# Softmax weights through diagonal matrices, six dense columns with an unsplit float32 second layer, one norm chain for three tiles

## The chip, the core and the metric

One core of a Trainium2 chip runs the kernel. The metric is the device time of one execution in microseconds (us). The engines are TensorE (PE, with its weight load PEld), VectorE (DVE), ScalarE (ACT), GpSimd (POOL) and the DMA queues; SP issues most transfers, POOL the gathers by index.

## The reference, cut to what matters

512 tokens of width 1024 pass through one decoder layer: attention with three branches beside a state-space group, then a layer in which each token chooses 128 of 16384 experts.

```
z = rms_norm(h, attn_norm);  proj = z @ w_in
p_s = masked_softmax(q @ k_sel);  p_w = masked_softmax(q @ k_win)
a = g0 * (p_c @ v_c) + g1 * (p_s @ v_sel) + g2 * (p_w @ v_win)
h = h + concat([a, s5(u)]) @ w_out
x = rms_norm(h, ffn_norm)
eidx, gate = top 16 of 256 key pairs, for each of 8 heads
act = gelu(x . u_tab[eidx]) * gate
h = h + sum over the chosen experts of act * v_tab[eidx]
out = rms_norm(h, final_norm)
```

## The kernel before

Tokens are cut into four tiles of 128 (`T` = 0 to 3).

**Attention.** `attention(T)` goes through four groups, two sets of heads `g` by two branches `br`. `scores` makes the scores of four heads, takes their maximum on DVE (`nm`), their exponential on ACT (`Pt`, with the sum `sm`), turns `sm` into gate over sum, and multiplies each head's `Pt` by it: on DVE for T < 3, on ACT for T = 3 (`PSC`). `pv` then takes 128 x 128 blocks of `Pt`, four heads to a PSUM bank, transposes them with the identity on PE, copies the bank to SBUF and multiplies by the values. There are T + 1 blocks for each head, so tile 1 has 32 transposes, tile 2 has 48, tile 3 has 64.

**Experts, two ways.** Tiles 0 and 1 (`SPARSE`) gather the rows of their chosen experts by index. A step takes one expert for each of 128 tokens: a gather of 1 MB, a dot product on DVE (`junk<-X`), a gelu on ACT, and a sum on DVE (`X<-X,act`) or, for the last 20 steps of tile 0, on PE by a diagonal matrix (`dg`, built on ACT from the identity, two matmuls a step). The 128 steps of tile 0 (`peer`) run between the attention and routing of tiles 1 to 3; the 128 of tile 1 (`Steps`) run in the dense loop, one a column.

Tiles 2 and 3 (`DENSE`) compute all 16384 experts in `dense`, 128 columns of 128 experts, with a gate of zero where an expert is not chosen. Column j loads two 512 KB halves (u and v) into a ring of three `raw` buffers, and splits each half into a float32r high part (`hi`, ACT) and low part (`lo`, DVE). The first layer (`hid`) is 24 matmuls of 256 columns. After gelu and gate the activations are split too (`acthi` on ACT, `actlo` on DVE), and the second layer (`outp`) is 12 float32r matmuls of 512 columns into four banks `acc` that stay open for the whole loop. A `raw` half is released, and the next load issued, when its `lo` is done. For j < 64 the gates of columns 64 to 127 are made beside the loop, one group every second column: one-hot tables on DVE, 16 small matmuls on PE.

**Order.** Before the loop the order on each engine comes from a scheduler. Inside it the order is the program's (`ordered`): iteration j holds `hid(j + 1)`, the step of tile 1, `gated(j + 1)`, `actlo(j + 1)`, `outp(j)`, `lo(j + 1, 1)`. An engine works in order; semaphores tie the engines together.

**End.** `final` is an RMS norm: a square with sum on ACT, then a chain of 14 small DVE operations (`rms`, with `rsqrt`), a scaling of 128 x 1024, and the store. Its small tiles (`f_s`, `f_r`) have two buffers, and three tiles (1, 2, 3) go through it after the loop.

Of the kernel before, what the change touches and what calls it, by code (L numbers as in the profile page):

```python
# [12 lines left out]
F32 = mybir.dt.float32  # L13
# [3 lines left out]
I32 = mybir.dt.int32  # L17
U32 = mybir.dt.uint32
AF = mybir.ActivationFunctionType
ALU = mybir.AluOpType  # L20
# [143 lines left out]
def hymba_kernel(ctx: ExitStack, tc: tile.TileContext, a, out, dbg=None):  # L164
# [520 lines left out]
    kcF, vcF = ct("kcF", [128, 2, 31]), ct("vcF", [31, 2, 64])  # L685


    PSC = lambda T, h: T > 2
    PCP = lambda T, kb: T < 3 and kb % 2
    AT, ST, XN, EI, GA = {}, {}, {}, {}, {}  # L690

    def attention(T):
        N = 128 * (T + 1)
        n31 = 7 if T == 0 else 31
        kcT, vcn = (kc0, vc0) if T == 0 else (kcF, vcF)
        ob = bank()
        O = b3(ob, 128)

        pcs = [bank(), bank()]
        for h in range(8):  # L700
            rows = slice(64 * (h % 2), 64 * (h % 2) + 64)
            PE.matmul(b3(pcs[h % 2], 128)[:, h // 2, 0:n31], qT[T][rows, h // 2], kcT[rows, h // 4], start=True, stop=True)
        scl = M.S()
        sc = scl.v([128, 8, n31])
        mx = tiny.tile([128, 8], F32, name="mx")
        sh = [128, 8, n31]
        for par in range(2):
            V.tensor_tensor(sc[:, par::2], b3(pcs[par], 128)[:, :, 0:n31], cmpb[:, T, 0:1, 0:n31].to_broadcast([128, 4, n31]), op=ALU.add)
        bfree(*pcs)
        V.reduce_max(mx, sc, axis=AX.X)  # L710
        V.tensor_tensor(sc, sc, mx[:, :, None].to_broadcast(sh), op=ALU.subtract)
        S.activation(sc, sc, AF.Exp)
        V.tensor_tensor(sc, sc, cmpb[:, T, 1:2, 0:n31].to_broadcast(sh), op=ALU.mult)
        V.reduce_sum(mx, sc, axis=AX.X)
        V.tensor_scalar(mx, mx, 1e-30, None, op0=ALU.max)
        V.reciprocal(mx, mx)
        V.tensor_tensor(mx, mx, gts[:, T, :, 0], op=ALU.mult)
        V.tensor_tensor(sc, sc, mx[:, :, None].to_broadcast(sh), op=ALU.mult)
        yield

        def scores(g, br):
            pl = M.S() if T == 0 else M.L((0, 1))
            Pt = pl.v([128, 4, N])
            nm = tiny.tile([128, 4], F32, name="nm")
            sm = tiny.tile([128, 4], F32, name="sm")
            for h in range(4):
                par, i = h % 2, h // 2
                ps = bank()
                rows = slice(64 * par, 64 * par + 64)
                PE.matmul(ps[:, 0:N], qT[T][rows, 2 * g + i], KT[rows, 2 * br + g, 0:N], start=True, stop=False)  # L730
                PE.matmul(ps[:, N - 128:N], identb, maskb, start=False, stop=True)
                V.reduce_max(nm[:, h:h + 1], ps[:, 0:N], axis=AX.X, negate=True)
                S.activation(Pt[:, h], ps[:, 0:N], AF.Exp, bias=nm[:, h:h + 1], accum_out=sm[:, h:h + 1])
                bfree(ps)
            V.tensor_scalar(sm, sm, 1e-30, None, op0=ALU.max)
            V.reciprocal(sm, sm)
            V.tensor_tensor(sm, sm, gts[:, T, 4 * g:4 * g + 4, 1 + br], op=ALU.mult)
            for h in range(4):
                if PSC(T, h):
                    S.activation(Pt[:, h], Pt[:, h], AF.Copy, scale=sm[:, h:h + 1])  # L740
                else:
                    V.tensor_scalar(Pt[:, h], Pt[:, h], sm[:, h:h + 1], None, op0=ALU.mult)
            return pl, Pt

        def pv(g, br, pl, Pt):
            for kb in range(T + 1):
                b = bank()
                pt = b3(b, 128)
                for h in range(4):
                    PE.transpose(pt[:, 2 * (h % 2) + h // 2], Pt[:, h, kb * 128:kb * 128 + 128], ident)  # L750
                ps = M.S()
                PT = ps.v([128, 4, 128])
                if PCP(T, kb):
                    V.tensor_copy(PT, pt)
                else:
                    S.activation(PT, pt, AF.Copy)
                bfree(b)
                for par in range(2):
                    PE.matmul(O[64 * par:64 * par + 64, 2 * g:2 * g + 2], VC[:, kb, 128 * br + 64 * g:128 * br + 64 * g + 64],
                              PT[:, 2 * par:2 * par + 2], start=(br == 0 and kb == 0), stop=False, skip_group_check=True)  # L760
                M.free(ps)
                yield
            M.free(pl)

        prev = None
        for g in range(2):
            for br in range(2):
                cur = (g, br) + scores(g, br)
                yield
                if prev:  # L770
                    yield from pv(*prev)
                    if prev[1] == 1:
                        yield from cmp_pv(prev[0], sc, vcn, O, n31)
                prev = cur
        yield from pv(*prev)
        yield from cmp_pv(1, sc, vcn, O, n31)
        M.free(scl)
        al = M.S()
        aT = al.v([128, 4, 128])
        S.activation(aT, O, AF.Copy)  # L780
        bfree(ob)
        AT[T] = (al, aT)
        tap(f"aT{T}", aT)
        yield
# [430 lines left out]
    def dense(xh, xl, sp):  # L1215
# [15 lines left out]
        def load(n):  # L1231
            if ring[n] and nload[n] < NE:
                raw, j = ring[n].popleft(), nload[n]
                nload[n] += 1
                SP.dma_start(raw, a["uvt"][j][:, half[n]])
                loaded[n][j] = raw

        def hi(j, n):
            if j < NE:
                S.activation(his[j % 2][:, half[n]], loaded[n][j], AF.Copy)  # L1240

        def lo(j, n):
            if j < NE:
                o = half[n]
                V.tensor_tensor(los[j % 2][:, o], loaded[n][j], his[j % 2].bitcast(F32)[:, o], op=ALU.subtract)
                ring[n].append(loaded[n].pop(j))
                load(n)

        def hid(j):
            if j < NE:  # L1250
# [16 lines left out]
                V.tensor_tensor(g, g, gates_of(j), op=ALU.mult)  # L1267

        def acthi(j):
            if j < NE:  # L1270
                S.activation(acts[j % 2][:, 0], gS[j % 2], AF.Copy)

        def actlo(j):
            if j < NE:
                act = acts[j % 2]
                V.tensor_tensor(act[:, 1], gS[j % 2], act.bitcast(F32)[:, 0], op=ALU.subtract)

        def outp(j):
            (ah, al), vh, vl = (acts[j % 2][:, i] for i in range(2)), his[j % 2][:, D:], los[j % 2][:, D:]
            for t in range(2):  # L1280
                ts = slice(128 * t, 128 * t + 128)
                for i, (l, r) in enumerate(((ah, vh), (ah, vl), (al, vh))):
                    for n in range(2):
                        PE.matmul(acc[2 * t + n], l[:, ts], r[:, 512 * n:512 * n + 512], start=(j == 0 and i == 0),
                                  stop=(j == NE - 1 and i == 2), skip_group_check=True)
# [23 lines left out]
        with ordered("V", "S", "PE", "G"):  # L1309
            gated(0)  # L1310
            acthi(0)
            actlo(0)
            next(ngp)
            for j in range(NE):
                gp, ngp = ngp, gate_group(j)
                step = sp.k < 128 and (j + 1) * n > done * SPREAD
                hi(j + 2, 0)
                hi(j + 1, 1)
                next(gp, None)
                next(ngp, None)  # L1320
                if step:
                    sp.dot()
                hid(j + 1)
                if step:
                    sp.gelu()
                lo(j + 2, 0)
                gelu(j + 1)
                next(gp, None)
                gated(j + 1)
                next(gp, None)  # L1330
                acthi(j + 1)
                if step:
                    sp.add()
                    done += 1
                actlo(j + 1)
                outp(j)
                lo(j + 1, 1)
                if sp.k == 128 and step:
                    final(sp.T, xs[sp.T], junk)
                if j == 100:  # L1340
                    for i in range(2):
                        SP.dma_start(row(7)[:, half[i]], hsave[i])
        assert sp.k == 128
        for i, T in enumerate(DENSE):
            xs[T] = row(7)[:, half[i]]
            for n in range(2):
                V.tensor_tensor(xs[T][:, 512 * n:512 * n + 512], acc[2 * i + n], xs[T][:, 512 * n:512 * n + 512], op=ALU.add)
            final(T, xs[T], raws[i][:, 0:D])


    proj_k(0, w_k[1], G)
# [299 lines left out]
```

## Time and profile before

| | us |
|---|---|
| median of three runs (1617.03 to 1622.68) | 1618.69 |
| profiled execution, its own time | 1620.03 |
| profiled execution, span from first to last instruction | 1618.2 |
| DVE busy | 1475.7 |
| PE busy | 1367.1 |
| ACT busy | 837.0 |

The span is what the trace covers; the time of the same execution is 1.8 us longer. Busy time counts an engine's instructions as they lie in the trace, where those that follow each other overlap a little.

### The profile page before, as it was taken

What the parts mean: (1) busy time and instruction counts of PE and PEld (TensorE: products, weight loads), DVE (VectorE), ACT (ScalarE), POOL (GpSimd) and SP (SyncE); (2) the same over time, 40 slices, a digit from 0 to 9 for tenths busy, and PEclk for the clock granted to TensorE, in tenths of its full rate; (3) what the DMA queues carried; (4) which work ended last, traced back from release to release, by engine and by line L of the source; (5) the groups of instructions that cost most, each with busy time, mean ns of one, the idle gap of its engine ahead of it and who ended that gap; (6) DMA issues with size and microseconds to landing.
All of it is one profiled execution on the core that took longest, in us unless ns stands there. A gap on an engine that the chain in (4) does not pass through costs nothing.

```text
span 1618.2 us, 24071 instructions
## 1 busy us (share of the span) xinstructions
PE 1367.1 (84%) x8256; PEld 1081.8 (67%) x8256; DVE 1475.7 (91%) x3392; ACT 837.0 (52%) x2046; POOL 521.8 (32%) x383
## 2 busy tenths in 40 slices
PE   5687794588946689696579999999999999999996
PEld 2366572454433455682358888888888999999995
DVE  8986279969899999699999999999999999999998
ACT  2335523545455675225565555555555556555553
POOL 6422013745354233003002333333333433333331
PEclk9897898787877789899859999999999999999998
DMA  6331478888998989309707999999999999999994
GB/s 263 104 105 65 169 278 295 330 321 300 375 352 297 345 356 370 152 6 343 248 4 262 338 345 332 342 337 340 333 346 357 392 375 377 374 375 379 375 376 171
DMA packets 88967, 469.45 MB, mean 290 GB/s; under 512 B 10253, under 2 KB 10893, under 8 KB 50701
## 3 DMA queue, kind: packets, MB, share of 16 engines
q0 software_dynamic: 37152, 268.98, 42.7%
q1 hardware_dynamic: 51692, 198.94, 34.3%
q8 instruction: 64, 1.05, 0.2%
q14 instruction: 59, 0.48, 0.1%
HBM read 464.74 MB, written 3.15 MB: 289 GB/s over the span
## 4 chain that ended last, share of the span: by engine, by line
DVE 46%; PE 29%; issue 12%; DMA 6%; ACT 3%; POOL 3%; SPq 0%; DVEq 0%; POOLq 0%; ACTq 0%
PE bank L134 29%; DVE X L134 27%; DVE lo L134 8%; DVE junk L134 7%; DMA X<-in_uv,eidx 5%; POOL X L134 2%; ACT X L134 2%; DVE act L134 1%; DVE nm L134 1%; DVE more L134 1%; DMA X<-in_x 0%; ACT gt L134 0%; DMA raw<-in_uvt 0%; DVE zT L134 0%; DVE hid L134 0%
## 5 line engine op out<-in xcount | busy, mean ns | idle before, releaser
L134 POOL DMA_INDIRECT X<-in_uv,eidx x256 | 431.6, 1686 | 967.0 <-DVE X L134 854.1
L134 ACT ACTIVATE X<-bank 128x256 f32<-128x256 f32 (+5 forms) x423 | 213.4, 518 | 184.0 <-PE bank L134 134.3
L134 PE MATMUL bank<-hi,act 128*128 128x512 f32 x1024 | 299.7, 394 | 0.0
L134 PE MATMUL bank<-XH,hi 128*128 128x256 f32 x1024 | 288.9, 282 | 4.1 <-ACT hi L134 4.1
L134 PE MATMUL bank<-XH,lo 128*128 128x256 f32 x1024 | 287.8, 281 | 0.0
L134 PE MATMUL bank<-XL,hi 128*128 128x256 f32 x1024 | 287.5, 281 | 0.0
L134 PE MATMUL bank<-X 128*128 128x64 f16 (+10 forms) x1768 | 235.9, 283 | 59.6 <-DVE X L134 39.7
L134 DVE CUSTOM_DVE_ANT_0 junk<-X 128x1024 bf16<-128x1024 f32 x206 | 250.8, 1217 | 14.0 <-DMA X<-in_uv,eidx 11.0
L134 ACT ACTIVATE gt<-hid 128x1 f32<-128x1 f32 x384 | 63.8, 198 | 363.1 <-DVE hid L134 362.9
L134 DVE TENSOR_TENSOR X<-X 128x256 f32<-128x256 f32 (+13 forms) x611 | 230.6, 410 | 22.5 <-ACT X L134 19.7
L134 DVE SCALAR_TENSOR_TENSOR X<-X,act 128x1024 f32<-128x1024 f32 x194 | 247.6, 1276 | 3.6 <-ACT act L134 3.6
L134 DVE TENSOR_TENSOR lo<-raw,hi 128x1024 fp32r<-128x1024 f32 x172 | 209.4, 1217 | 2.8 <-ACT hi L134 2.8
L134 PEld LDWEIGHTS bank<-hi,act 128*128 128x128 f32 x1024 | 183.3, 188 | 32.6
L134 PEld LDWEIGHTS bank<-XH,hi 128*128 128x128 f32 x1024 | 193.9, 189 | 9.1 <-ACT hi L134 4.2
L134 PEld LDWEIGHTS bank<-XL,hi 128*128 128x128 f32 x1024 | 193.3, 189 | 4.9
L134 PE MATMUL bank<-X,X 128*128 128x128 f32 (+7 forms) x888 | 177.1, 373 | 20.9 <-ACT X L134 12.9
L134 PEld LDWEIGHTS bank<-XH,lo 128*128 128x128 f32 x1024 | 194.2, 190 | 0.0
L134 ACT ACTIVATE hi<-raw 128x1024 fp32r<-128x1024 f32 x172 | 179.0, 1053 | 27.4 <-PE bank L134 21.8
L134 PEld LDWEIGHTS bank<-X,X 128*128 128x128 f32 (+4 forms) x888 | 119.8, 194 | 66.2 <-issue 29.7
L134 PE MATMUL bank<-lo,act 128*128 128x512 f32 x512 | 159.5, 393 | 0.4 <-DVE lo L134 0.4
L134 PEld LDWEIGHTS bank<-X 128*128 128x128 f32 (+3 forms) x744 | 117.5, 197 | 54.9 <-issue 28.5
L134 PE MATMUL bank<-c_ident,X 128*128 128x128 f32 (+2 forms) x300 | 55.6, 337 | 85.4 <-DVE X L134 49.4
(202 smaller groups left out, 1775.2 us busy)
## 6 DMA issues: line engine op xcount, KB each, us to landing
raw<-in_uvt SPq DMA_DIRECT2D x172, 512.0 KB, 7.0
X<-in_uvt SPq DMA_DIRECT2D x84, 512.0 KB, 6.7
X<-in_wq SPq DMA_DIRECT2D x24, 1024.0 KB, 8.9
X<-in_wo SPq DMA_DIRECT2D x8, 1024.0 KB, 7.7
X<-in_x SPq DMA_DIRECT2D x8, 512.0 KB, 3.7
X<-in_wB SPq DMA_DIRECT2D x4, 1024.0 KB, 12.8
X<-in_wA SPq DMA_DIRECT2D x4, 1024.0 KB, 5.2
X<-in_w SPq DMA_DIRECT2D x4, 1024.0 KB, 5.5
```

Of the source, the lines that this page charges most:

```text
L134: ins = self.last = f(*args, **kw)
```

## The change

The attention of tiles 1 to 3 no longer scales `Pt`. For each head ACT builds a 128 x 128 diagonal matrix `dl` from the identity and `sm`, and PE multiplies the block of `Pt` by `dl` in an ordinary float32 matmul, which transposes and scales at once. Tile 0 stays as it was. The four `dl` of a group take one small slot, allocated in `scores` and freed in `pv`.

In columns 4, 14, 24, 34, 44 and 54 (`whole`) the v half and the activations are not split: `hi`, `lo`, `acthi` and `actlo` are left out there, and `outp` is 4 float32 matmuls that read `raw` itself. The `raw` half of such a column is released after `outp(j)` in iteration j, where otherwise `lo(j, 1)` releases it in iteration j - 1.

After the loop, the three sums of squares go into one [128, 3] tile, one chain of 14 operations serves the three tiles, and the scalings and stores are cut into halves of 512 columns.

```
-    PSC = lambda T, h: T > 2
...
+            dl = None if T == 0 else M.S()
             for h in range(4):
-                if PSC(T, h):
-                    S.activation(Pt[:, h], Pt[:, h], AF.Copy, scale=sm[:, h:h + 1])
+                if T == 0:
+                    V.tensor_scalar(Pt[:, h], Pt[:, h], sm[:, h:h + 1], None, op0=ALU.mult)
                 else:
-                    V.tensor_scalar(Pt[:, h], Pt[:, h], sm[:, h:h + 1], None, op0=ALU.mult)
+                    S.activation(dl.v([128, 4, 128])[:, h], ident, AF.Copy, scale=sm[:, h:h + 1])
...
-                    PE.transpose(pt[:, 2 * (h % 2) + h // 2], Pt[:, h, kb * 128:kb * 128 + 128], ident)
+                    o, p = pt[:, 2 * (h % 2) + h // 2], Pt[:, h, kb * 128:kb * 128 + 128]
+                    if T == 0:
+                        PE.transpose(o, p, ident)
+                    else:
+                        PE.matmul(o, p, dl.v([128, 4, 128])[:, h], start=True, stop=True)
...
+        def whole(j):
+            return j < JC and j % 10 == 4
...
         def hi(j, n):
-            if j < NE:
+            if j < NE and not (n and whole(j)):
...
         def lo(j, n):
-            if j < NE:
+            if j < NE and not (n and whole(j)):
...
         def acthi(j):
-            if j < NE:
+            if j < NE and not whole(j):
...
         def actlo(j):
-            if j < NE:
+            if j < NE and not whole(j):
...
         def outp(j):
+            if whole(j):
+                for t in range(2):
+                    for n in range(2):
+                        PE.matmul(acc[2 * t + n], gS[j % 2][:, 128 * t:128 * t + 128], loaded[1][j][:, 512 * n:512 * n + 512],
+                                  start=False, stop=False, skip_group_check=True)
+                done_with(j, 1)
+                return
...
-                if sp.k == 128 and step:
-                    final(sp.T, xs[sp.T], junk)
...
+        s2, r1, r2, ri = (dtab.bitcast(F32)[:, 0, 4 * i:4 * i + 3] for i in range(4))
+        S.activation(junk, xs[sp.T], AF.Square, accum_out=s2[:, 2:3])
...
-            final(T, xs[T], raws[i][:, 0:D])
+            S.activation(raws[i][:, 0:D], xs[T], AF.Square, accum_out=s2[:, i:i + 1])
+        V.tensor_scalar(s2, s2, 1.0 / D, EPS, op0=ALU.mult, op1=ALU.add)
+        rsqrt(r2, s2, r1, ri)
+        for n in range(2):
+            for i, T in ((2, sp.T), (0, DENSE[0]), (1, DENSE[1])):
+                o = slice(512 * n, 512 * n + 512)
+                V.scalar_tensor_tensor(xs[T][:, o], xs[T][:, o], r2[:, i:i + 1], fn[:, o], op0=ALU.mult, op1=ALU.mult)
+                SP.dma_start(out[T * 128:(T + 1) * 128, o], xs[T][:, o])
```

The places where the order on an engine moves follow. On ACT, after the exponentials of the first group of tile 1 (`X,sm<-bank,nm`; `gt` and `act` belong to the steps of tile 0), there stood before:

```order
L134 ACTIVATE X,sm<-bank_86,nm 128x256
L134 ACTIVATE act<-gt 128x1
L134 ACTIVATE gt<-hid 128x1 x2
L134 ACTIVATE gt<-hid,ga_1303 128x1
L134 ACTIVATE gt<-gt,hid 128x1
L134 ACTIVATE act<-gt 128x1
L134 ACTIVATE X,sm<-bank_89,nm 128x256
L134 ACTIVATE X,sm<-bank_90,nm 128x256
L134 ACTIVATE X,sm<-bank_87,nm 128x256
L134 ACTIVATE X,sm<-bank_86,nm 128x256
```

and with the change there stand:

```order
L134 ACTIVATE X,sm<-bank_86,nm 128x256
L134 ACTIVATE act<-gt 128x1
L134 ACTIVATE X_77<-c_ident,sm 128x128 x4
L134 ACTIVATE X,sm<-bank_89,nm 128x256
L134 ACTIVATE X,sm<-bank_90,nm 128x256
L134 ACTIVATE gt<-hid 128x1 x2
L134 ACTIVATE gt<-hid,ga_1303 128x1
L134 ACTIVATE X,sm<-bank_87,nm 128x256
L134 ACTIVATE gt<-gt,hid 128x1
L134 ACTIVATE act<-gt 128x1
```

The four diagonal matrices (`X_77<-c_ident,sm`) come ahead of the next group's exponentials and of the next step's gelu.

On DVE, around the end of the iteration ahead of column 4 (`lo` and `act` are the low parts, `junk` and the `X` after it belong to the gate tables), there stood before:

```order
L134 TENSOR_TENSOR X<-X 128x256
L134 SCALAR_TENSOR_TENSOR X<-X,act 128x1024
L134 TENSOR_TENSOR act_5364<-X,act_5364 128x256
L134 TENSOR_TENSOR lo_5361<-raw_5359,hi_5360 128x1024
L134 TENSOR_TENSOR junk<-X 128x512
L134 TENSOR_TENSOR X<-junk,X 128x512 x2
L134 ISA junk,hid<-X 128x1024
L134 ISA hid 128x1
L134 TENSOR_TENSOR lo_5361<-raw_5358,hi_5360 128x1024
L134 TENSOR_TENSOR X<-X 128x256
L134 SCALAR_TENSOR_TENSOR X<-X,act 128x1024
```

and with the change there stand:

```order
L134 TENSOR_TENSOR X<-X 128x256
L134 SCALAR_TENSOR_TENSOR X<-X,act 128x1024
L134 TENSOR_TENSOR junk<-X 128x512
L134 TENSOR_TENSOR X<-junk,X 128x512 x2
L134 ISA junk,hid<-X 128x1024
L134 ISA hid 128x1
L134 TENSOR_TENSOR lo_5361<-raw_5358,hi_5360 128x1024
L134 TENSOR_TENSOR X<-X 128x256
L134 SCALAR_TENSOR_TENSOR X<-X,act 128x1024
```

Between the sum of tile 1's step and the gate tables `act_5364` and `lo_5361<-raw_5359` are gone.

On PE, in the second layer of column 4 (banks 85, 89, 86 and 84 are `acc`), there stood before:

```order
L134 MATMUL bank_85<-hi_5360,act_5364 128x512
L134 MATMUL bank_89<-hi_5360,act_5364 128x512
L134 MATMUL bank_85<-lo_5361,act_5364 128x512
L134 MATMUL bank_89<-lo_5361,act_5364 128x512
L134 MATMUL bank_85<-hi_5360,act_5364 128x512
L134 MATMUL bank_89<-hi_5360,act_5364 128x512
L134 MATMUL bank_86<-hi_5360,act_5364 128x512
L134 MATMUL bank_84<-hi_5360,act_5364 128x512
L134 MATMUL bank_86<-lo_5361,act_5364 128x512
L134 MATMUL bank_84<-lo_5361,act_5364 128x512
L134 MATMUL bank_86<-hi_5360,act_5364 128x512
L134 MATMUL bank_84<-hi_5360,act_5364 128x512
```

and with the change there stand, behind the last gate matmul:

```order
L134 MATMUL bank_87<-X 128x64
L134 LDWEIGHTS X
L134 MATMUL bank_87<-X 128x64
L134 MATMUL bank_85<-raw_5359,X 128x512
L134 MATMUL bank_89<-raw_5359,X 128x512
L134 MATMUL bank_86<-raw_5359,X 128x512
L134 MATMUL bank_84<-raw_5359,X 128x512
```

Twelve instructions that read `hi`, `lo` and `act` have become four that read `raw` and the gated activations (`X`).

## Rows read from the trace of the kernel before

**Rows 1.** Page, chain that ended last, by engine.

```profile
DVE 46%; PE 29%; issue 12%; DMA 6%; ACT 3%; POOL 3%; SPq 0%; DVEq 0%; POOLq 0%; ACTq 0%
```

**Rows 2.** Busy time by stage: from:to, length, engine busy (instructions), PEclk, DMA share, GB/s.

```profile
340.00:660.00 320.00, 236.18 (x1065) 140.98 (x1064) 297.23 (x719) 178.59 (x632) 123.65 (x91) 0.80 0.88 338
870.00:1238.00 368.00, 357.30 (x2608) 321.71 (x2607) 365.98 (x534) 207.04 (x385) 122.05 (x60) 1.00 0.93 339
1240.00:1594.00 354.00, 354.00 (x2279) 321.81 (x2279) 341.31 (x446) 209.99 (x383) 128.09 (x63) 1.00 0.97 376
```

**Rows 3.** Waits of DVE in 340 to 660: us, times, longest.

```profile
DVE junk L134 <- DMA X<-in_uv,eidx: 7.9, 3, 4.0
```

**Rows 4.** Waits of PE in 340 to 660.

```profile
PE bank L134 <- DVE X L134: 51.4, 8, 22.3
```

**Rows 5.** Timeline of DVE, one scaling of tile 1, one of tile 2.

```profile
385.17 1.12 DVE L134 TENSOR_SCALAR X<-X,sm 128x256 f32<-128x256 f32 x4
...
498.94 1.40 DVE L134 TENSOR_SCALAR X<-X,sm 128x384 f32<-128x384 f32 x4
```

**Rows 6.** Groups of ACT, shapes apart: busy us, mean ns, idle before.

```profile
L134 ACT ACTIVATE X<-X,sm 128x512 f32<-128x512 f32 x16 | 10.2, 710 | 2.3 <-DVE sm L134 2.2
L134 ACT ACTIVATE dg<-c_ident,act 128x128 f32<-128x128 f32 x20 | 8.0, 399 | 1.6 <-PE bank L134 1.1
```

**Rows 7.** PE: one group, then three timeline rows at full clock.

```profile
L134 PE MATMUL bank<-X,dg 128*128 128x512 f32 x80 | 38.5, 612 | 16.8 <-ACT dg L134 16.8
...
424.81 7.03 PE L134 MATMUL bank<-X,X 128*128 128x512 f32 x16
...
471.40 5.58 PE L134 MATMUL bank<-X,X 128*128 128x128 f32 x48
...
481.26 2.50 PE L134 MATMUL bank<-c_ident,X 128*128 128x128 f32 x20 [1.28 <-DVE X L134]
```

**Rows 8.** Timeline of PE, end of attention of tile 3.

```profile
586.74 3.68 PE L134 MATMUL bank<-c_ident,X 128*128 128x128 f32 x16 [4.73 <-ACT X L134]
592.18 5.50 PE L134 MATMUL bank<-X,X 128*64 128x256 f32 x30 [1.76 <-ACT X L134]
597.51 1.04 PE L134 MATMUL bank<-c_ident,X 128*128 128x128 f32 x8
```

**Rows 9.** Timeline of DVE, end of a column in the first half.

```profile
1111.66 0.42 DVE L134 TENSOR_TENSOR act<-X,act 128x256 fp32r<-128x256 f32 x1
...
1113.13 0.42 DVE L134 TENSOR_TENSOR junk<-X 128x512 f16<-128x512 f16 x1
```

**Rows 10.** Chain in order of time, around the middle of the dense loop.

```profile
1221.92 1.61 DVE X L134 x2
1234.34 1.61 DVE X L134 x2
1238.60 358.26 PE bank L134 x2319
```

**Rows 11.** PE in the dense loop: timeline, then its waits in 870 to 1238.

```profile
1109.02 1.08 PE L134 MATMUL bank<-hi,act 128*128 128x512 f32 x4
...
PE bank L134 <- DVE X L134: 6.5, 29, 0.2
```

**Rows 12.** DMA issues in 870 to 1235: count, KB, median us to landing.

```profile
raw<-in_uvt SPq DMA_DIRECT2D x79, 512.0 KB, 5.5
```

**Rows 13.** Timeline of the end, ACT then DVE.

```profile
1603.96 1.06 ACT L134 ACTIVATE junk<-X 128x1024 bf16<-128x1024 f32 x1 [1.86 <-DVE X L134]
...
1607.59 1.06 ACT L134 ACTIVATE raw<-X 128x1024 f32<-128x1024 f32 x1 [1.44 <-DVE f_r L134]
...
1603.85 1.28 DVE L134 TENSOR_TENSOR X<-bank,X 128x512 f32<-128x512 f32 x2
...
1612.86 0.16 DVE L134 TENSOR_TENSOR f_r<-f_r,f_r 128x1 f32<-128x1 f32 x1
1613.05 1.28 DVE L134 SCALAR_TENSOR_TENSOR X<-X,f_r 128x1024 f32<-128x1024 f32 x1
```

More of the change, by code (lines that the diff above doesn't have):

```diff
@@ L737, in scores, with pv @@
             V.tensor_tensor(sm, sm, gts[:, T, 4 * g:4 * g + 4, 1 + br], op=ALU.mult)
+            dl = None if T == 0 else M.S()
             for h in range(4):
-                if PSC(T, h):
-                    S.activation(Pt[:, h], Pt[:, h], AF.Copy, scale=sm[:, h:h + 1])
-                else:
-                    V.tensor_scalar(Pt[:, h], Pt[:, h], sm[:, h:h + 1], None, op0=ALU.mult)
-            return pl, Pt
-        def pv(g, br, pl, Pt):
+                if T == 0:
+                    V.tensor_scalar(Pt[:, h], Pt[:, h], sm[:, h:h + 1], None, op0=ALU.mult)
+                else:
+                    S.activation(dl.v([128, 4, 128])[:, h], ident, AF.Copy, scale=sm[:, h:h + 1])
+            return pl, Pt, dl
+        def pv(g, br, pl, Pt, dl):
             for kb in range(T + 1):
@@ L762, in pv @@
                 yield
-            M.free(pl)
+            M.free(pl, *([dl] if dl else []))
         prev = None
@@ L1236, in load, with done_with @@
                 loaded[n][j] = raw
+        def whole(j):
+            return j < JC and j % 10 == 4
         def hi(j, n):
-            if j < NE:
+            if j < NE and not (n and whole(j)):
                 S.activation(his[j % 2][:, half[n]], loaded[n][j], AF.Copy)
+        def done_with(j, n):
+            ring[n].append(loaded[n].pop(j))
+            load(n)
         def lo(j, n):
-            if j < NE:
+            if j < NE and not (n and whole(j)):
                 o = half[n]
                 V.tensor_tensor(los[j % 2][:, o], loaded[n][j], his[j % 2].bitcast(F32)[:, o], op=ALU.subtract)
-                ring[n].append(loaded[n].pop(j))
-                load(n)
+                done_with(j, n)
         def hid(j):
@@ L1343, in dense @@
         assert sp.k == 128
+        s2, r1, r2, ri = (dtab.bitcast(F32)[:, 0, 4 * i:4 * i + 3] for i in range(4))
+        ri = ri.bitcast(I32)
+        S.activation(junk, xs[sp.T], AF.Square, accum_out=s2[:, 2:3])
         for i, T in enumerate(DENSE):
```

## The prediction

> **What bounds the kernel now.** I read the chain by engine first: DVE holds 46% of it, PE 29%, ACT 3% [rows 1]. So work taken from DVE can shorten the kernel, work taken from ACT hardly. The change touches three places, and the busy time by stage says what limits each [rows 2]. In the attention of tiles 1 to 3 (340 to 660) DVE is busy 297 of 320 us, PE 236, ACT 179: DVE leads, PE has 84 us idle. In the first half of the dense loop (870 to 1238) DVE is busy 366 of 368 us and PE 357, at a granted clock of 1.00: DVE bounds, PE is close behind. In the second half (1240 to 1594) PE is busy all 354 us. The chain agrees: it steps along DVE X every 12.42 us (two columns) up to 1238.6, and from there lies on PE for 358 us [rows 10]. Transfers move 339 GB/s in the first half and 376 in the second [rows 2], so the first half could run some 10% faster before it asks for more than the second half gets.
>
> What sets each stage's margin is read from the waits. PE's idle time in the attention is mostly one wait: for DVE X, 51.4 us in 8 pieces [rows 4]. DVE itself waits little there; its longest named wait, for gathered rows, is 7.9 us in three pieces [rows 3]. In the dense loop's first half PE waits for DVE X 29 times, 6.5 us in all [rows 11]: 0.22 us in each pair of columns, which is all the room it has.
>
> **How many passes a float32 matmul makes.** Both new uses of PE are ordinary float32 matmuls. The 20 steps of tile 0 that are summed on PE are 40 matmuls in the code, and the trace holds 80 records of them, all of one shape [rows 7]: one matmul leaves two records. At full clock a record of 512 columns takes 7.03/16 = 0.44 us, one of 128 columns 5.58/48 = 0.116 us, and a transpose by the identity 2.50/20 = 0.125 us [rows 7]. The transposes of the code leave one record each. So a transpose that becomes a matmul goes from 0.12 to 0.23 us: +0.11 us at full clock, +0.23 at half. A float32r column costs 358.26 us / 64 columns / 12288 = 0.456 ns (24 matmuls of 256, 12 of 512) [rows 10], 0.233 us for 512.
>
> The Trainium skill, "FP8 and Floating Point Precision", section "TensorE Precision Notes", says that true float32 makes four passes through the array. Four passes at a float32r record's 0.233 us would be 0.93 us per matmul of 512 columns, an estimate; two records of 0.44 are 0.88, so this trace bears the rule out, and it speaks against the change: whoever took a record for a whole matmul would see the second layer become cheaper on PE.
>
> **Part 1, attention.** Removed: eight groups of four scalings on DVE, 4 x 1.12 us for tile 1 and 4 x 1.40 us for tile 2 [rows 5], 10.1 us, in a stretch where DVE is busy 93%: 9.4 us of the path at most. On ACT tile 3 replaces 16 scalings of 0.71 us by 16 diagonals of 0.40 [rows 6], -5.0 us, while tiles 1 and 2 add 32 diagonals, +12.8 us. ACT is busy 56% of the stretch, and a group of four (1.6 us) takes the place of a DVE group of 1.1 to 1.4 us between `sm` and the first block: behind it on ACT wait the next exponentials and a gelu, for whose result DVE waits. I take that at nothing; uncovered it is 8 x 1.6 = 12.8 us.
>
> PE: 144 transposes (32, 48, 64) get a second record: 16 us at full clock, 33 us at half. The cover is the 51.4 us in which PE waits for DVE X. For tiles 1 and 2 the 80 extra records are 8.8 us at full clock; spread over eight groups, most lie in that wait, and I let a quarter through, 2.4 us. For the end of tile 3 there is no cover: 16 transposes at 586.74 took 3.68 us (0.23 each, so half clock), with a wait of only 1.76 us for ACT behind them [rows 8]. They would take 3.7 us more, less that wait, less the 1.24 us by which ACT's four operations are shorter: +0.7. The next 16, at 0.13 us (8 in 1.04), get 1.8 more [rows 8]. Together +2.5 us. Part 1: -9.4 + 2.4 + 2.5 = **-4.5 us**, between -9.4 (all extra passes hidden) and +23.7 (all exposed at half clock).
>
> A diagonal also takes a small slot, so gather buffers shift and the scheduler orders some steps anew; no row gives this a price. The stretch's gather waits bound it: 7.9 us either way [rows 3].
>
> **Part 2, six whole columns.** All six are in the DVE-bound half. Removed from DVE: `actlo` and the v half's `lo`, from 1111.66 to 1113.13, 1.47 us a column [rows 9]. ACT loses two conversions; it is busy 207 of 368 us [rows 2], worth nothing. PE: 4 matmuls x 2 records x 0.44 = 3.52 us in place of 12 x 0.233 = 2.80, +0.7 us. Take ten columns, one of them whole. DVE: 62.1 - 1.47 = 60.6 us. PE: 5 x (12.42 - 0.22) + 0.7 = 61.7 us. PE takes over as the bound: 0.4 us less than 62.1, times six **-2.4 us**. DVE's lead of 1.47 us is used up at 0.22 us a pair, about the 10 columns to the next whole one. Bounds: -8.8 if DVE alone decided (6 x 1.47), +4.2 if PE's waits could not be pulled in (6 x 0.7).
>
> The `raw` half of a whole column is released about 4 us later, after `outp(j)`, so the next v load into it is late by as much; behind it on SP's queue stands the next u load. A load lands 5.5 us after issue [rows 12], and three buffers give it about two columns, 12.4 us, so 9.5 fits. Taken at nothing; uncovered some 4 us each, 24 us.
>
> **Part 3, the end.** Three squares start on ACT as their sums arrive; the last sum on DVE ends at 1603.85 + 1.28 = 1605.13 [rows 13]. Before, the third square waited 1.44 us for a buffer of `f_r`, until 1607.59, and its own chain and a scaling of 1.28 us followed, to 1614.33 [rows 13]. After: square 1605.15 to 1606.4 with its readout, 14 steps of 0.19 us (1612.86 to 1613.05 [rows 13]) to 1609.1, six half scalings of 0.64 us to 1612.9. **-1.4 us**; bounds 0 (a late square or more cost of three columns) and -2.4 (the wait plus a shorter last store).
>
> **Sum.** -4.5 - 2.4 - 1.4 = -8.3 us. The profiled execution took 1620.03 us (span 1618.2), so 1611.7; the median is 1.3 us lower, so **1610.5 us**.
>
> **Rivals.**
> A, the forecast: 1607 to 1614.5, as the exposed share of the extra passes goes from a little less to more. Chance 0.47.
> B, all extra passes hide behind the waits for DVE X, part 1 gives -9.4: 1618.7 - 13.2 = 1605.5. For it: 51.4 us of waits against 16. Against it: the end of tile 3 has no such wait [rows 8]. 0.20.
> C, part 1 gives nothing, since the diagonals hold up ACT's exponentials and gelus or gathers shift: 1618.7 - 3.8 = 1614.9. For it: a group of four stands ahead of a gelu in ACT's order. 0.16.
> D, slower: the second pass is exposed at half clock in the transposes of tiles 1 and 3, 96 x 0.23 = 22.1 us, less 9.4: +12.7, with parts 2 and 3 1627.6. For it: the mean granted clock of the stretch is 0.80, and the transposes at 586.74 ran at 0.23 us each after a wait of 4.73 us [rows 8]. Against it: most waits of PE are for DVE, which gets shorter. It decides from 9.4 + 3.8 + 4.9 = 18.1 us exposed, more than all passes cost at full clock. 0.07.
> E, a matmul of `raw` leaves one record and not two: PE gets cheaper, DVE alone decides, part 2 gives -8.8, 1604.1. Against it the 80 records for 40 matmuls. 0.04.
> F, part 2 doesn't gain: PE's short waits sit where the extra 0.7 us can't use them, +4.2: 1617.1. For it: PE's orders are fixed, and a whole column needs `gS` and a `raw` that it holds longer. 0.06.
>
> **How the numbers follow.** 0.3% (4.9 us) is about what a measurement of this kernel can tell from no change: faster means under 1613.8, slower over 1623.5. A (nine tenths of it), B and E give faster: 0.66. The rest of A, C and F give the same: 0.27. D gives slower: 0.07. The range 1603 to 1619 holds A, B, E, F and most of C; it leaves out D, the ends of C by gathers, and a B with more than its price.
>
> **What would show it.** Right: in 340 to 660 DVE loses about 10 us of busy time and PE gains 16 to 33, its wait for DVE X shrinks; the dense loop's first half is 2 to 3 us shorter, with PE at 98% or more and DVE below 99%; columns 4, 14, ... show 8 records of 512 columns; from the last sum to the last scaling takes 7.8 us in place of 9.2. Wrong: PE's matmuls by `dl` with waits for ACT X in front of them and half clock (C or D); a DVE wait for `raw` after a whole column (F or worse); 4 records a whole column (E); new waits of DVE for gathers (the order of the scheduler).

## The result and the profile after

| | median us | runs | ratio to before, 95% interval |
|---|---|---|---|
| before, beside the first runs | 1620.68 | 4 | |
| changed | 1601.47 | 4 (1600.04 to 1605.59) | 0.9878 (0.9854 to 0.9903) |
| changed, run again beside the experiments | 1603.81 | 6 | 0.9874 (0.9842 to 0.9905) |

The change is worth 1.2%, some 20 us, where I forecast 8, and the time lies below my range. The profiled execution is the slowest of the first four, 1605.59 us, span 1603.8, so the trace has 14.4 us to explain. By stage, in the columns of [rows 2] (the dense stretches are cut where they lie now):

```profile
340.00:660.00 320.00, 253.89 (x1232) 159.37 (x1232) 288.18 (x693) 180.64 (x658) 122.34 (x91) 0.82 0.88 336
870.00:1226.00 356.00, 351.68 (x2569) 311.06 (x2569) 353.93 (x517) 198.67 (x368) 116.93 (x59) 1.00 0.95 347
1250.00:1584.00 334.00, 334.00 (x2157) 303.88 (x2156) 321.62 (x420) 197.21 (x362) 123.39 (x59) 1.00 0.96 372
```

In the attention DVE lost 9 us of busy time and PE gained 18, as forecast; PE's wait for DVE X, which was to shrink, did not (51.4 us before [rows 4], 53.4 now). In the first dense stretch DVE stayed full (353.93 of 356 us), where I had named less than 99% as a sign of being right, and PE is now nearly full as well.

A mark in each dense column places the gain: the gelu, ACT's only `X<-bank 128x256`. Columns 1 and 64 in the timeline of ACT, first in the kernel before:

```profile
855.25 1.39 ACT L134 ACTIVATE X<-bank 128x256 f32<-128x256 f32 x2
...
1245.57 0.36 ACT L134 ACTIVATE X<-bank 128x256 f32<-128x256 f32 x1
```

and in the changed kernel:

```profile
849.93 1.41 ACT L134 ACTIVATE X<-bank 128x256 f32<-128x256 f32 x2
...
1231.87 0.36 ACT L134 ACTIVATE X<-bank 128x256 f32<-128x256 f32 x1
```

Column 1 comes 5.32 us earlier: that is what lies ahead of the loop, with the attention in it. Column 64 comes 13.70 us earlier: the dense first half gave 8.4 us, in six steps of 1.4, each in the iteration of a whole column and none in between. Around column 65 a late load cost 0.7 us net, and the end gave the rest. The rows of the end, DVE in the changed kernel, answer to [rows 13]:

```profile
1590.87 1.28 DVE L134 TENSOR_TENSOR X<-bank,X 128x512 f32<-128x512 f32 x2
...
1593.36 0.37 DVE L134 TENSOR_SCALAR X<-X 128x3 f32<-128x3 f32 x2 [1.22 <-ACT raw L134]
...
1596.14 4.07 DVE L134 SCALAR_TENSOR_TENSOR X<-X 128x512 f32<-128x512 f32 x6
```

From the last sum (1592.15) to the last scaling (1600.21) it takes 8.06 us in place of 9.20, and the span ends 3.6 us later in place of 3.9: -1.4 us, as the sum had it. So -5.3 - 8.4 + 0.7 - 1.4 = -14.4. The late load at column 65 belongs to this execution: the same kernel run again (e4) does not show it.

The dense loop repeats closely from one profile to the next: columns 1 to 64 take 390.31 to 390.46 us in the fifteen profiles without whole columns there. The part ahead of it does not repeat. Five profiles (before, e1, e3, e9, e10) hold the same instructions ahead of the loop in the same order on DVE, ACT and, as far as its records go, PE, and their column 1 comes at 851.6 to 857.3 us; in the changed kernel, e2 and e4, which are alike in this too, it comes at 849.9, 843.8 and 850.8. So a few us in one profile ahead of the loop say little, the 5.32 above among them; the times of many runs weigh more there.

PE at column 4 of the changed kernel, in its timeline (gate matmuls, the float32 second layer, the first two of the next `hid`):

```profile
872.43 0.65 PE L134 MATMUL bank<-X 128*128 128x64 f16 x16
872.92 3.68 PE L134 MATMUL bank<-raw,X 128*128 128x512 f32 x8
876.04 0.68 PE L134 MATMUL bank<-XH,hi 128*128 128x256 f32 x1
876.56 0.28 PE L134 MATMUL bank<-XL,hi 128*128 128x256 f32 x1
```

Eight records for four matmuls, as said. They hold PE from 872.92 to about 876.44 (one 0.12 us step ahead of 876.56): 3.52 us, as forecast.

### The profile page after: what moved, and what is told of

It reads as the page before. It is cut to its first block, busy times and chain, and to the rows that moved or that the text cites. A ratio compares the mean times of both kernels' runs of the same rounds, so it can differ in the third digit from the quotient of the medians.

```text
span 1603.8 us, 24233 instructions
## 1 busy us (share of the span) xinstructions
PE 1382.1 (86%) x8376; PEld 1090.4 (68%) x8376; DVE 1455.6 (91%) x3323; ACT 832.2 (52%) x2066; POOL 523.9 (33%) x383
## 4 chain that ended last, share of the span: by engine, by line
DVE 25%; PE 21%; issue 4%; DMA 1%; ACT 1%; SPq 0%; DVEq 0%; ACTq 0%
PE bank L134 21%; DVE X L134 12%; DVE lo L134 8%; DVE junk L134 3%; DVE act L134 1%; DMA raw<-in_uvt 1%; ACT X L134 0%; DVE hid L134 0%; ACT hi L134 0%; ACT raw L134 0%; SPq L1240 0%; DVE more L134 0%; ACT act L134 0%; DVEq L1674 0%; DVE ab L134 0%
## 5 line engine op out<-in xcount | busy, mean ns | idle before, releaser
L134 ACT ACTIVATE X<-bank 128x256 f32<-128x256 f32 (+5 forms) x431 | 218.4, 520 | 188.4 <-PE bank L134 136.5
L134 PE MATMUL bank<-X 128*128 128x64 f16 (+10 forms) x1816 | 249.7, 289 | 65.5 <-DVE X L134 50.0
L134 PE MATMUL bank<-hi,act 128*128 128x512 f32 x976 | 285.2, 394 | 0.0
L134 DVE TENSOR_TENSOR X<-X 128x256 f32<-128x256 f32 (+15 forms) x636 | 236.3, 405 | 24.1 <-ACT X L134 21.0
L134 PE MATMUL bank<-X,X 128*128 128x128 f32 (+5 forms) x1172 | 214.6, 358 | 23.1 <-ACT X L134 12.9
L134 PEld LDWEIGHTS bank<-X,X 128*128 128x128 f32 (+3 forms) x1172 | 152.8, 198 | 71.2 <-issue 30.3
L134 PEld LDWEIGHTS bank<-hi,act 128*128 128x128 f32 x976 | 174.7, 188 | 30.8
L134 PEld LDWEIGHTS bank<-X 128*128 128x128 f32 (+3 forms) x792 | 126.8, 197 | 72.6 <-issue 32.4
L134 PE MATMUL bank<-lo,act 128*128 128x512 f32 x488 | 151.9, 392 | 0.8 <-DVE lo L134 0.8
L134 PEld LDWEIGHTS bank<-lo,act 128*128 128x128 f32 x488 | 91.4, 188 | 22.4 <-DVE lo L134 1.7
```

What stands on the lines that cost most here:

```text
L134: ins = self.last = f(*args, **kw)
```

## The experiments

Each ratio is to the kernel before on the same chip (medians 1618.8 to 1622.2 us), with its 95% interval; microseconds are the change in the ratio times that median.

**The parts alone.** Each kernel is the one before with one part of the diff.

e1, the six whole columns. 

> Only the six whole columns. Theory 1 (PE has more room than its waits show: a pair of columns needs 2 x 5.59 us, the second half's period, plus 0.49 for the 16 gate matmuls, 11.67 of 12.42 us, so DVE alone decides): -8.6 us, six times 1.44, each gained in the iteration of the whole column. Theory 2 (the forecast's room of 0.22 us a pair): -2.4 us, and PE is the bound in the pairs behind a whole column.

Ratio 0.9944 (0.9924 to 0.9963), -9 us. Columns 1 and 64, ACT's timeline:

```profile
854.17 1.41 ACT L134 ACTIVATE X<-bank 128x256 f32<-128x256 f32 x2
...
1236.13 0.36 ACT L134 ACTIVATE X<-bank 128x256 f32<-128x256 f32 x1
```

381.96 us where before had 390.32: -8.36, that is 1.39 for each whole column, gained in the iterations of the whole columns. This is theory 1.

e2, the diagonals in tiles 1 to 3. 

> Only the diagonal matrices in the attention of tiles 1 to 3. The forecast's sum: -4.5 us. If all the extra passes are hidden: -9.4 us. If the diagonals hold up ACT and PE: 0 or more.

Ratio 0.9922 (0.9903 to 0.9942), -12.6 us (-15.7 to -9.4): at or beyond the -9.4 of all of DVE's relief.

e3, the end. 

> Only the joint norm chain at the end. The forecast's sum: -1.4 us, read from the last sum to the last scaling (7.8 us in place of 9.2). If the end hides nothing: 0.

Ratio 0.9988 (0.9973 to 1.0003), -2 us, not told from none by the times; the timeline of the end above carries the reading. In this kernel's own profile it takes 8.06 us again from the last sum to the last scaling, and from the last column's gelu to the end of the span 1.8 us less than before (19.53 in place of 21.30).

e4, all three again. 

> The changed kernel again. If the three parts add: the sum of the three kernels run beside it, with theory 1 some -8.6 - 4.5 - 1.4 = -14.5 us; if the median gain of 19 us of the first runs holds, some 4.5 us come from the parts together and from none alone.

Ratio 0.9874 (0.9842 to 0.9905), -20 us; the parts alone sum to -24. They add, within the intervals.

**Where the room on PE ends, and what a whole column costs.** `whole` is altered in the kernel with the columns alone.

```
-            return j < JC and j % 10 == 4
+            return 0 < j < JC and j % 2 == 0         # e9
+            return j >= JC + 6 and j % 10 == 4       # e10
```

e9. 

> Only whole columns, but 31 of them (every even column from 2 to 62). Theory 1 (PE needs 11.67 us of a pair's 12.42, and a whole column adds 0.7): PE becomes the bound at 12.37 us a pair, -1.5 us in all. The forecast's room of 0.22 us a pair: 12.90 us a pair, +15 us. Were the float32 matmuls cheap and DVE alone the limit: -45 us.

Ratio 1.0225 (1.0185 to 1.0265), +36 us: none of the three. Waits of ACT in the first half of the loop, 870 to 1240 (us, times, longest):

```profile
ACT hi L134 <- DMA raw<-in_uvt: 88.9, 17, 6.1
ACT hi L134 <- DMA X<-in_uvt: 41.0, 8, 5.7
```

The chain of e9:

```profile
1223.41 1.15 DVE lo L134
1224.62 0.33 SPq L1235
1224.99 9.07 DMA raw<-in_uvt
1234.15 1.06 ACT hi L134
```

`hi` now waits 130 us for loads, and the chain runs from a `lo` over SP's issue and a load of 9 us to the next `hi`. So loads bound this kernel. That the late release of the whole columns' halves, which I had taken at nothing, puts them there, with too few ordinary columns between in which the loads catch up, is the likely reason; no run releases the halves earlier, so it is not shown. The kernel does not tell PE's room.

e10. 

> Only six whole columns, but in the second half of the loop (74, 84, ... 124), where PE is the bound. Price of the float32 matmuls by the forecast (8 records of 0.44 us for 12 of 0.233): +0.7 us each, +4.2 us. Were a matmul one record: -6 us. Were the late v half the point: about the gain of the first half, -8 us.

Ratio 1.0029 (1.0008 to 1.0050), +4.7 us. Columns 75 to 77 in ACT's timeline, with whole column 74 behind the first mark:

```profile
1302.70 0.38 ACT L134 ACTIVATE X<-bank 128x256 f32<-128x256 f32 x1 [1.35 <-PE bank L134]
...
1308.96 0.38 ACT L134 ACTIVATE X<-bank 128x256 f32<-128x256 f32 x1 [1.05 <-PE bank L134]
...
1314.54 0.38 ACT L134 ACTIVATE X<-bank 128x256 f32<-128x256 f32 x1 [0.37 <-PE bank L134]
```

6.26 us and then 5.58: a whole column costs +0.68 us where PE is the bound. Six make 4.1. The forecast's price of 0.7 was right, and no gain comes from the late v half.

**Taking the attention apart.** In e5 only tile 3 has diagonals, in e6 only tiles 1 and 2; e7 has none and scales all three tiles on ACT; e8 is the kernel before with its transposes made twice.

```
     PSC = lambda T, h: T > 2
+    DG = (3,)                     # e5
+    DG = (1, 2)                   # e6
-    PSC = lambda T, h: T > 2
+    PSC = lambda T, h: T > 0      # e7
...
+    for _ in range(1 if T == 0 else 2):                   # e8
         PE.transpose(pt[:, 2 * (h % 2) + h // 2], ...)
```

e5. 

> Diagonals in tile 3 only (64 transposes become matmuls; ACT builds 16 diagonals of 0.40 us in place of 16 scalings of 0.71; DVE unchanged). Theory 1 (the forecast): +2.5 us, the second pass lies open at the end of tile 3's attention. Theory 2 (ACT's scaling stood on the path of the last groups, and the shorter diagonal gives back more than the second pass takes): -2 to -5 us.

Ratio 1.0032 (1.0011 to 1.0054), +5.2 us (+1.8 to +8.8): theory 1, whose +2.5 lies in the interval.

e6. 

> Diagonals in tiles 1 and 2 only; tile 3 scales on ACT as before. The forecast: -9.4 us of DVE + 2.4 us of extra passes = -7.0. All of DVE's relief and hidden passes: -9.4. If tile 3 gives the rest of the measured -12.6 us of the attention: this kernel -8 to -10, the one beside it -3 to -4.

Ratio 0.9916 (0.9894 to 0.9939), -13.6 us (-17.2 to -9.9): more than all three, the last of them at the edge of the interval.

e7. 

> No diagonals: the scalings of tiles 1 and 2 go from DVE to ACT (32 of some 0.5 to 0.6 us), the transposes stay. It takes the same 10.1 us from DVE with no second pass on PE. If the second passes cost what the forecast says for tiles 1 and 2 (2.4 us): 2 us better than diagonals in tiles 1 and 2. If they are hidden and ACT's longer operations are not: some 2 to 4 us worse, -5 to -7 against before.

Ratio 0.9963 (0.9945 to 0.9981), -6.0 us (-8.9 to -3.1), less than half of what the diagonals gave in theirs.

e8. 

> The kernel before with each transpose of tiles 1 to 3 made twice into the same place: one record more for each, 144 x 0.115 us at full clock, as the second pass of a float32 matmul, and nothing else changed but the scheduler's view of it. The forecast: +4.9 us. If PE's waits for DVE hide them: 0, within 2 us. All exposed at half clock: +33 us.

Ratio 1.0060 (1.0038 to 1.0082), +9.7 us (+6.2 to +13.3): in this order the second pass is dearer than my 4.9.

**Is it DVE's relief, the slot, or the order?** e11 leaves out the scaling of tiles 1 and 2 but for one column.

```
-  V.tensor_scalar(Pt[:, h], Pt[:, h], sm[:, h:h + 1], None, op0=ALU.mult)
+  c = N if T == 0 else 1
+  V.tensor_scalar(Pt[:, h, 0:c], Pt[:, h, 0:c], sm[:, h:h + 1], None, op0=ALU.mult)   # e11
```

e11. 

> The kernel before with the scalings of tiles 1 and 2 cut to their first column: left out is the scaling of the others. It takes some 8 of the 10.1 us from DVE and touches neither PE nor ACT. DVE's busy share as the price (the forecast): -7 to -9 us. If the relief of DVE alone explains the -13.6 us of the diagonals in tiles 1 and 2: -11 to -14. If the diagonals themselves shorten something (order, the wait for ACT): -5 to -9, and the rest is theirs.

Ratio 0.9998 (0.9978 to 1.0018): nothing. The 32 operations that are left still take 4.4 us of DVE, where the whole scalings took 10.2, so DVE's relief is smaller than the 8 us that I expected. The stretch from the first exponential of tile 1 to the last of tile 3, and from there to column 1, in the columns of [rows 2], for the kernel before:

```profile
355.36:583.55 228.19, 167.59 (x728) 95.63 (x726) 214.38 (x448) 128.02 (x473) 93.88 (x63) 0.78 0.85 321
583.55:855.25 271.70, 212.23 (x1283) 150.88 (x1284) 246.25 (x999) 133.50 (x358) 38.94 (x35) 0.85 0.53 203
```

for e3, whose instructions ahead of the loop are those of before:

```profile
353.84:585.99 232.15, 175.84 (x727) 101.01 (x724) 214.13 (x448) 128.61 (x474) 94.03 (x63) 0.74 0.85 314
585.99:857.28 271.29, 214.83 (x1282) 152.05 (x1283) 246.08 (x999) 133.60 (x358) 40.02 (x35) 0.84 0.53 204
```

for e11:

```profile
350.51:576.61 226.10, 172.32 (x728) 100.23 (x726) 202.40 (x439) 123.98 (x459) 82.63 (x60) 0.76 0.82 309
576.61:855.01 278.40, 215.54 (x1282) 152.32 (x1283) 253.11 (x1008) 136.66 (x373) 46.30 (x38) 0.82 0.54 210
```

and for e6:

```profile
354.71:571.98 217.27, 176.26 (x816) 102.91 (x815) 197.61 (x418) 133.44 (x485) 81.53 (x58) 0.80 0.84 319
571.98:845.39 273.41, 212.51 (x1277) 149.55 (x1276) 254.61 (x997) 135.82 (x380) 45.74 (x40) 0.82 0.56 216
```

In the five profiles with the instructions of before the attention takes 228.2 to 232.4 us and the stretch behind it 270.7 to 271.7. In e11 DVE's busy time in the attention falls by 12 us (214.4 to 202.4) and the attention by only 2 to 6 (to 226.1). What was moved comes back later, where DVE has 7 us more to do and the stretch is 7 us longer. In e6 the attention is 11 to 15 us shorter, and 8 us of extra work afterwards lengthen the stretch by only 2 to 3. Over both stretches DVE is busy for 460.6 us before, 455.5 in e11 and 452.2 in e6: the diagonals take 8.4 us from DVE, the cut scalings 5.1. Waits of DVE in e11, 340 to 855 (us, times, longest):

```profile
DVE X L134 <- PE bank L134: 20.3, 6, 15.5
DVE nm L134 <- PE bank L134: 12.1, 11, 3.4
```

`nm`, the maximum over a bank of scores, waits 12.1 us for PE; in the profile of before it was 4.8, but in the five with its instructions it is 4.6 to 9.0. So a new wait for PE's scores may have taken the place of the work, but only 3 us of it stand out from what one order shows by itself.

e13 to e18 ask what slot and order do; each lets the scheduler make a new order. A slot taken and freed unused is `dl = None if T in (0, 3) else M.S()`; the trifling copy is

```
+            if T == 1:
+                V.tensor_copy(nm, sm)
```

e13. 

> The kernel before with the slot that the diagonals would take, for tiles 1 and 2, taken and freed but never used: no instruction is added, buffers and order shift. If the slot makes the gain: -5 to -13 us. If the diagonals do: 0, within 3.

Ratio 1.0017 (0.9999 to 1.0035), +2.8 us (-0.2 to +5.7): no gain from the slot in this order.

e14. 

> The unused slot, and the scalings of tiles 1 and 2 cut to their first column (the scaling of the others is left out). If slot and DVE's relief together make the gain: -11 to -14 us as with the diagonals. If the diagonals themselves do: 0, as without the slot.

Ratio 0.9963 (0.9946 to 0.9980), -6.0 us (-8.8 to -3.2): between the two.

e15. 

> The kernel before with one copy of 128 x 4 on DVE in each group of tile 1 (four in all, some 0.3 us of work): the scheduler orders thousands of rows anew. If the order alone moves the time: 3 us or more either way. If not: 0, within 3.

Ratio 1.0010 (0.9991 to 1.0028), +1.6 us (-1.5 to +4.5): within 3.

e16. 

> Diagonals in tiles 1 and 2 with the same copy. If the -13.6 us belong to the diagonals: -11 to -16 again. If they were a lucky order: much less, down to the 0 of the kernel with DVE's scalings cut.

Ratio 0.9947 (0.9931 to 0.9962), -8.6 us (-11.2 to -6.2): between the two.

e17. 

> Diagonals in tiles 1 and 2, built from head 3 down to head 0: the same work in a third order. If diagonals are worth more than DVE's relief whatever the order: -8 to -14 us. If their gain was the order's: between 0 and -6, as with the scalings cut.

Ratio 0.9918 (0.9889 to 0.9947), -13.3 us (-18.0 to -8.6), in the range of the first. (Tile 3's scalings on ACT run in the reversed order too.)

e18. 

> The scalings of tiles 1 and 2 cut to their first column (the scaling of the others is left out), with the copy of 128 x 4: a third order of this work. DVE's relief by itself has given 0 and -6.0: again between these if it is worth some 3 us; -9 or more if the first two were unlucky orders.

Ratio 0.9948 (0.9928 to 0.9967), -8.4 us (-11.7 to -5.3), beyond both earlier orders of this work.

Three orders of each kind: diagonals in tiles 1 and 2 gave -13.6, -8.6 and -13.3 us (mean -11.8), the scalings cut gave 0, -6.0 and -8.4 (mean -4.8). The same scalings cut stand 8 us apart in two orders, with intervals that do not touch; slot and copy by themselves gave +2.8 and +1.6 us, neither told from none. Of the 7 us between the two means, 3 to 4 are DVE's relief, which was larger with diagonals: its busy time over the two stretches falls by 8.4 to 8.9 us with diagonals in tiles 1 and 2, by 4.9 to 5.3 with the scalings cut. The rest lies in DVE's idle time over the same stretches, and there the orders overlap: 33, 38 and 41 us with diagonals, 36, 44 and 49 with the scalings cut, 38 to 43 in the five profiles of before. So a gain of the diagonals beyond DVE's relief is not shown.

**A better version.** The changed kernel with tile 3 scaled on ACT again and `j % 6 == 4`, ten whole columns.

e12. 

> The changed kernel with two alterations: tile 3 scales on ACT again (no diagonals there), and ten whole columns (4, 10, ... 58) in place of six. By theory 1 ten columns give -14.4 us (PE at 11.90 of 11.93 us a pair), diagonals in tiles 1 and 2 -13.6, the end -1.5: -29 us against before, some 8 us better than the changed kernel. By the forecast's room PE is the bound: -7 us for the columns.

The median is 1589.79 us, the ratio 0.9809 (0.9778 to 0.9840), -31 us. Columns 1 and 64, ACT's timeline:

```profile
842.41 1.41 ACT L134 ACTIVATE X<-bank 128x256 f32<-128x256 f32 x2
...
1219.47 0.37 ACT L134 ACTIVATE X<-bank 128x256 f32<-128x256 f32 x1
```

377.06 us, 13.3 less than before: 1.1 short of ten times 1.44, 0.6 of them lost at column 7, but far from the -7 of the forecast's room. The chain over this stretch now lies on PE, but for one load of 8.5 us ahead of column 7 that starts when PE has read the half of whole column 4:

```profile
853.15 15.90 PE bank L134 x111
869.07 8.52 DMA raw<-in_uvt
...
889.62 340.60 PE bank L134 x2464
```

## Why the prediction was wrong

**The step that failed first** is the term of part 2: PE's room, "0.22 us in each pair of columns, which is all the room it has". I took it from the list of waits, which counts only the time in which PE had no instruction running by the modelled ends of its matmuls. The starts tell another tale. PE in the timeline of before, the last `hid` matmul, the gate matmuls and the second layer:

```profile
877.58 0.28 PE L134 MATMUL bank<-XH,lo 128*128 128x256 f32 x1
878.07 0.94 PE L134 MATMUL bank<-X 128*128 128x64 f16 x16 [0.21 <-DVE X L134]
878.85 0.70 PE L134 MATMUL bank<-hi,act 128*128 128x512 f32 x2
```

The `hid` matmuls start 0.12 us apart, so the gate matmuls could have started at 877.70 and started at 878.07: 0.37 us. They took 0.78 us to the second layer, where the changed kernel's, with their tables long there, take 0.49 (872.43 to 872.92). That is 0.66 us, and the sum was to be had another way: two columns of the second half, where PE is the bound, at 5.59 us each, plus 0.49 for the gates, are 11.67 us of 12.42, 0.75 us of room. Then PE needs 5 x 11.67 + 0.7 = 59.1 us of ten columns with one whole, DVE 60.6, and DVE alone decides: six times 1.47, -8.8 us, measured -8.4 in place of my -2.4. With this term right, the sum would have come to some 1604 us, inside my range. It is the number of rival E, by another mechanism: the records are two for a matmul, not one, and the price was 0.68 to 0.7 us. The mechanism of part 2, DVE's relief against PE's room, was right, one term in it mis-sized. That the loads stay hidden held for six columns in 64, cost 0.6 us in one place among ten, and did not hold for 31.

**Part 1** was too small as well: -12.6 us alone (-15.7 to -9.4), where I had -4.5. DVE's relief held its price in the mean: the scalings cut took 5.1 us of busy time from DVE and gave 4.8 in the mean of three orders, 0.94 of it, where I had reckoned with 0.93; single orders gave 0 to -8.4. For tile 3 the +2.5 lies within the measured +5.2 (+1.8 to +8.8). The term that failed is the +2.4 for the second passes of tiles 1 and 2 (a slip besides: a quarter of 8.8 is 2.2). Diagonals there took some 8.5 us of busy time from DVE and gained 11.8 in the mean of three orders, so no cost of the second passes shows in them, and some 3 us more than the relief stand there, which the spread of the orders does not tell from none. Nor are second passes free by themselves: twice the transposes cost +9.7 us in one order. Scaling on ACT without diagonals gave -6.0 in its one order, the unused slot no gain in its one. What offsets the second passes stays open.

One candidate stands in the profiles and was not tested: the granted clock. These are the attention of e2 and then of the changed kernel, with the same instructions ahead of the loop:

```profile
353.41:569.05 215.64, 175.02 (x862) 107.57 (x862) 201.28 (x417) 132.15 (x495) 89.10 (x61) 0.83 0.87 326
```

```profile
353.65:576.40 222.75, 180.49 (x862) 110.31 (x862) 202.10 (x419) 132.54 (x494) 87.33 (x61) 0.80 0.85 317
```

7 us lie between them, at a mean granted clock of 0.83 and 0.80. In the seven profiles with diagonals in tiles 1 and 2 this clock is 0.80 to 0.83, in twelve others 0.73 to 0.79, and 0.80 with the transposes made twice. So a higher clock comes with the diagonals and may give back some of what their passes cost. No run holds the clock still, so this is not shown.

**Part 3** came as forecast: -1.4 in the profile, -1.4 to -1.8 in the four that have it. **The sum**: of the 11 us that the medians show beyond the forecast, 6 are part 2; the other 5 are left for part 1, by subtraction.

**Rivals.** B had its size near the truth for part 1; its reason, hidden passes, fits e6, e16 and e17, but e8 speaks against it. C, D and F did not come; exposed passes, the mechanism of D, show in e5 and e8, well below its 22 us.

## What to carry to other kernels

To find an engine's room in a loop, take its period where it is the bound (two columns at 5.59 us here), add what the other stretch asks of it besides (0.49), and compare with the period there (12.42); the list of waits shows only the time in which nothing ran. Where a scheduler sets the order, a run with a part left out is one draw: add a trifling instruction and measure the spread before a difference of 5 us is given a cause. Check in the trace what a left-out part really took away: the cut scalings freed 5 us of DVE, the diagonals 8.5. A buffer released an iteration late cost next to nothing for six and ten columns of 64; with every second column late, loads became the bound.

## What the runs showed of the hardware

A float32 matmul of 512 columns costs 0.88 us at a granted clock of 1.00 also with a freshly loaded `raw` as its operand (3.52 us for four), a float32r one 0.233. The Trainium skill ("FP8 and Floating Point Precision", section "TensorE Precision Notes") states that true float32 makes four passes. Four times 0.233 would be 0.93 us, an estimate; the measured 0.88 agrees to within 6%.

Executions of the same instructions differ in the granted clock of the attention, and in its length with it. With the instructions of before it takes 228.2 us in both profiles with a mean clock of 0.78 and 0.79, and 231.5 to 232.4 us in the three with 0.74 and 0.75; each mean is a mixture of the two levels, 1.2 and 2.4 GHz. No run isolates what the clock is worth.
